# Hybrid decoder layer on one core: a set's own block in four tiles of its own, the second chain's first blocks unit by unit, and turns in two steps

## The chip, the cores and the metric

The kernel runs on one core of a Trainium2 chip. The metric is device time in microseconds (us), the time from the start to the end of one execution on the chip; lower is better. The engines are named as in the profile: PE multiplies matrices (PEld is its weight load), DVE and ACT work on tiles, POOL and SP mainly issue DMAs here, and POOL also does a few tiny powers.

## What is computed

One decoder layer on a sequence of 256 tokens with 2048 channels, all float32. Cut to what matters:

```python
h = rmsnorm(x, pre_norm_g)
proj = h @ w_in                       # one wide projection, split into the parts below
o_a = gla_chunked(a_q, a_k, a_v, gk)  # gated linear attention, 4 heads
y_a = (rmsnorm(o_a, gla_norm_g) * silu(a_g)) @ w_branch_a
o_b = diff_attention(b_q, b_k, b_v, lam)   # 16 heads, two softmaxes each
y_b = (rmsnorm(o_b, diff_norm_g) * silu(b_g)) @ w_branch_b
merged = sigmoid(m_a) * y_a + sigmoid(m_b) * y_b
out = x + rmsnorm(merged @ w_out, post_norm_g)
```

Nearly all of the work is the weight matrices: every weight is read once from HBM, split into a rounded part `hi` and a rest `lo`, and multiplied with the activations, which are split in the same way: hi by hi, hi by rest, rest by hi.

## The kernel before

**Units.** The weights go through the kernel in units of half a load. `schedule()` lists 452 units in the order in which PE takes them. `take()` hands PE one unit and prepares (`emit_half`) those up to four further on: `AHEAD = 4`. A regular unit is half of a 1 MB tile `raw` (three buffers), loaded by SP (L277). ACT makes `hi` of it (L298), DVE makes `lo` (L299), each in one of three buffers; PE then multiplies (L463, or L484 and L486 for channel-major parts).

**Sets.** Ten 512-column parts of the projection are computed in five pairs, "sets" 0 to 4, by seven products of half size in place of eight (a Strassen scheme). Each product has four units, and a set's 28 units are mixed in between the regular ones (the tuples in `steps`). ACT and DVE split a set unit in lines L259 and L260, PE multiplies it in L657. The blocks of weights that the products need are sums and differences of blocks. They are kept in two chains of four tiles of 512 KB: POOL loads a block into a chain tile (L213) or adds one to what is there (L211, an accumulating DMA), and DVE adds one chain tile to the other (L224). `refill()` is called when a unit is prepared; it puts the next load of the same tile on the list `refills`, from which it is issued two set units later.

The products of a set are p1, q3, p5, q6, q7, p2, p4 in sets 0, 3 and 4 and p1, q3, p5, p2, q6, q7, p4 in sets 1 and 2 (`MOVED`). One of them, p2, uses a block as it is, its "own block". In the kernel before, p2's block is loaded by SP in two halves of 1 MB into the same three `raw` buffers that the regular units use (L253, tile `raw_s`), and it is asked for when unit p2.0 or p2.2 is prepared. In sets 0, 3 and 4 DVE then adds it to a chain tile (L229), which p4 reads.

**Where these units stand.** In the list of units: v2 is units 16 to 23, v3 24 to 31, v4 32 to 44. `start_sets()` runs when unit 26 is prepared (while PE takes unit 22) and asks for the first blocks of set 0, p1 and q3, eight loads in a row; it does the same for set 1 at unit 173. Set 0's p1 units are 33, 35, 38 and 40, its q3 units 43, 45, 47 and 50, its p2 units 81 to 89. Set 3's q6 units are 312 to 318, its p2 units 328 to 334, in turn with units of y00 and y01. Set 4's q6 units are 368 to 374, in turn with units of y03; then come its four q7 units in a row (376 to 379), and p2 from 381 on.

**Buffers.** `u()` takes one of the 34 buffers of 4 KB per partition in the pool `big`; chain tiles, the split activations `xs`, the split sums `square`, the values `vh` and `vl`, the branch inputs `oah`, `oal`, `obh`, `obl` and the merged result `mh`, `ml` all live there. A buffer comes free when its tile's last reader is done. PSUM has eight banks, shared by everything.

**Order.** Each engine works through its own queue in order. The order in each queue is not written by hand: when the program is built, the framework takes for each engine the first instruction of the program that it works out to be ready, so an instruction can stand ahead of others that come earlier in the program. A wrong guess about when a load lands or a matmul ends is then fixed in the queue. `tc.keep_in_program_order` and `tc.issue_after` pin single instructions; the loads and refills of the chains are not pinned.

**v2 to v4.** After each of these parts `evacuate()` copies two PSUM banks, scaled, to `vh` (ACT, L556) and `vl` (DVE, L557). v2 holds columns 816 to 1231, so 208 of its columns end a tile `vh` and 208 begin the next one; only v2 has pieces of 208 columns. The forget gate's four PSUM banks are copied to `gp` by ACT (L532).

**The end.** `y1` is computed in four parts, y10 to y13, of eight units each. After y11 four small tasks run between the units (`pump`, after every second unit): `joined(0)` and `joined(1)` merge the first two parts, and `turn(g)` turns part g by eight transposes on PE (L1157) into two PSUM banks, from which ACT (L496) and DVE (L497) make `mh` and `ml`. Part 2 is turned by the task `turned(2)` in y13, part 3 by `turned(3)` in o0. Then the output projection o0 to o3 reads `mh` and `ml`.

Of the kernel before, what the change touches and what calls it, by code (L numbers as in the profile page):

```python
# [14 lines left out]
P = 128  # L15
# [125 lines left out]
def order_of(n):  # L141
    return ORDERS[n not in MOVED]
# [3 lines left out]
def hybrid_kernel(ctx: ExitStack, tc, xt, xn, preg, postg, w, w2, gkb, glag, lamv, diffg, ident_d, causal_d, lmask_d, out):  # L146
# [12 lines left out]
    def u(shape, name, dtype=F32):  # L159
        count[0] += 1  # L160
        return big.tile(shape, dtype, tag="u", name=f"{name}_{count[0]}")
# [9 lines left out]
    def ps(tag):  # L171
        count[0] += 1
        return psum.tile([P, 512], F32, tag="bank", name=f"{tag}_{count[0]}")
# [5 lines left out]
    def f32(ap):  # L179
        return ap.bitcast(F32)  # L180
# [13 lines left out]
    chains = [[], []]  # L194
# [3 lines left out]
    def piece(key, q):  # L198
        size = sizes[key]
        at = begins[key] + q * size * P  # L200
        return w[at : at + P * size].rearrange("(p n) -> p n", p=P)

    refills = []

    def block(n, name, unit, add=True):

        _, chain, (kh, g) = PRODUCTS[name]
        src = piece(SETS[n][g], 2 * kh + unit // 2)[:, 1024 * (unit % 2) : 1024 * (unit % 2) + 1024]
        dst = chains[(chain + n) % 2][unit]
        if add:  # L210
            pool.dma_start(dst, src, accum_op=ALU.add)  # L211
        else:
            pool.dma_start(dst, src)  # L213

    def refill(i, n, name, unit, raw):

        late = lambda *args, **kw: refills.append((i + 2, args, kw))
        x, y = chains[n % 2][unit], chains[(n + 1) % 2][unit]
        if name == "p1":
            late(n, "p5", unit)  # L220
        elif name == "p5" and n in MOVED:
            late(n, "q6", unit)
        elif name == "p5":
            dve.tensor_tensor(out=x, in0=x, in1=y, op=ALU.add)  # L224
            late(n, "q7", unit)
        elif name == "p2" and n in MOVED:
            late(n, "q7", unit)
        elif name == "p2":
            dve.tensor_tensor(out=x, in0=x, in1=raw, op=ALU.add)  # L229
        elif name == "q6" and n in MOVED:  # L230
            late(n, "p4", unit)
        elif name == "q7" and 0 < n < len(SETS) - 1:
            late(n + 1, "p1", unit, add=False)
        elif name == "p4" and 0 < n < len(SETS) - 1:
            late(n + 1, "q3", unit, add=False)
        while refills and refills[0][0] <= i:
            _, args, kw = refills.pop(0)
            block(*args, **kw)

    def emit_half():  # L240
        j = emitted[0]
        emitted[0] += 1
        key, unit = steps[j]
        if j in begin:
            start_sets()
        if isinstance(key, int):
            i = set_steps.index((key, unit))
            name, part = order_of(key)[unit // 4], unit % 4
            _, chain, (kh, g) = PRODUCTS[name]
            if chain is None:  # L250
                if part % 2 == 0:
                    raws[key] = wpool.tile([P, 2048], F32, tag="raw", name=f"raw_s{key}_{unit}")
                    sp.dma_start(raws[key], piece(SETS[key][g], 2 * kh + part // 2))  # L253
                raw = raws[key][:, 1024 * (part % 2) : 1024 * (part % 2) + 1024]
            else:
                raw = chains[(chain + key) % 2][part]
            hi_t = wpool.tile([P, 1024], F32R, tag="hi", name=f"hi_{j}")
            lo_t = wpool.tile([P, 1024], F32R, tag="lo", name=f"lo_{j}")
            act.activation(hi_t, raw, AF.Copy)  # L259
            dve.tensor_tensor(out=lo_t, in0=raw, in1=f32(hi_t), op=ALU.subtract)  # L260
            refill(i, key, name, part, raw)
            ready[j] = ((key, unit), hi_t, lo_t)
            return
        size = sizes[key]
        h = unit % 2
        src = piece(key, unit // 2)
        if h == 0:
            raws[key] = wpool.tile([P, 2048], F32, tag="raw", name=f"raw_{key}_{unit}")
        raw = raws[key]
        n = size // 2  # L270
        early = key == "v0"
        if h == 0:
            if j == 0:
                load_x(0, 1)
            cuts = (0, n, size) if j == 0 else (0, size)
            for a, b in zip(cuts, cuts[1:]):
                i = sp.dma_start(raw[:, a:b], src[:, a:b])  # L277
                if early:
                    tc.keep_in_program_order(i)
                if j == 0 and a == 0:  # L280
                    load_x(1, 3)
            if early:
                for kt in X_LOADS[j // 2]:
                    load_x(kt, 4)
        if early:
            prep_x(j)
            if 6 <= j < 14:
                square_x(j - 6)
        if key == "o3" and j + 1 < len(steps):
            hi_t, lo_t = u([P, 1024], "keep", F32R), u([P, 1024], "keep", F32R)  # L290
        else:
            hi_t = wpool.tile([P, 1024], F32R, tag="hi", name=f"hi_{j}")
            lo_t = wpool.tile([P, 1024], F32R, tag="lo", name=f"lo_{j}")
        fine = 2 if j == 0 else 1
        for i in range(fine):
            a, b = n * i // fine, n * (i + 1) // fine
            r = raw[:, n * h + a : n * h + b]
            act.activation(hi_t[:, a:b], r, AF.Copy)  # L298
            dve.tensor_tensor(out=lo_t[:, a:b], in0=r, in1=f32(hi_t[:, a:b]), op=ALU.subtract)  # L299
        ready[j] = (key, hi_t, lo_t)  # L300
# [23 lines left out]
    def load_x(kt, n):  # L324
        tc.keep_in_program_order(sp.dma_start(xraw[kt // 4][:, kt % 4 : kt % 4 + n, :], xt[:, kt : kt + n, :]))
# [4 lines left out]
    def prep_x(kt):  # L330
        i, j = kt // 4, kt % 4
        src = xraw[i][:, j, :]
        g = preg_s[:, kt : kt + 1]
        hi, lo = x_ops(kt)
        act.activation(hi, src, AF.Copy, scale=g)
        dve.scalar_tensor_tensor(out=lo, in0=src, scalar=g, in1=f32(hi), op0=ALU.mult, op1=ALU.subtract)
# [3 lines left out]
    def square_x(i):  # L340
        src = xraw[i // 2][:, 2 * (i % 2) : 2 * (i % 2) + 2, :].rearrange("p a t -> p (a t)")
        t = t2([P, 512], "xsq") if i else ssum
        tc.keep_in_program_order(act.activation(t, src, AF.Square))
        if i:
            dve.tensor_tensor(out=ssum, in0=ssum, in1=t, op=ALU.add)
# [149 lines left out]
    def split_out(bank, hi, lo, gain):  # L495
        act.activation(hi, bank, AF.Copy, scale=gain)  # L496
        dve.scalar_tensor_tensor(out=lo, in0=bank, scalar=gain, in1=f32(hi), op0=ALU.mult, op1=ALU.subtract)  # L497
# [125 lines left out]
    def start_sets():  # L623
        n = started[0]
        started[0] += 1
        while "squares" not in done:
            with tc.issue_after(latest[0]):
                next(operands, None)
        if n:
            for name, far in parts_far.items():  # L630
                parts[name] = tuple(u([P, 8, P], "square", F32R) for _ in far)
                for t, src in zip(parts[name], far):
                    pool.dma_start(f32(t), src)
        for c in range(2):
            chains[c][:] = [u([P, 1024], f"chain{c}") for _ in range(4)]
        for name in ("p1", "q3"):
            for unit in range(4):
                block(n, name, unit, add=False)

    def block_set(n, use):  # L640

# [87 lines left out]
    def late():  # L729
        norm_row()  # L730
        yield
        lam()
        yield
# [401 lines left out]
    first, both, raw = {}, {}, {}  # L1135
# [15 lines left out]
    def turn(g):  # L1151
        for i in range(2):
            bank = ps("bg")
            for j in range(2):
                for b in range(2):
                    c = P * (2 * i + j)
                    pe.transpose(bank[:, P * (2 * j + b) : P * (2 * j + b) + P], both[g][:, b, c : c + P], ident)  # L1157
            hi = mh[g][:, 2 * i : 2 * i + 2, :].rearrange("p a t -> p (a t)")
            lo = ml[g][:, 2 * i : 2 * i + 2, :].rearrange("p a t -> p (a t)")
            split_out(bank, hi, lo, 0.5)  # L1160

    def joined(g):
        yield from first_part(g)
        t = both[g]
        dve.scalar_tensor_tensor(out=t, in0=t, scalar=1.0, in1=raw[g], op0=ALU.add, op1=ALU.mult)
        dve.tensor_tensor(out=t, in0=t, in1=first[g], op=ALU.add)
        yield
        turn(g)

    def turned(g):  # L1170
        yield
        turn(g)

    for g in range(4):
        banks = token_major(f"y1{g}", 512, b_ops, 4)
# [145 lines left out]
```

## Time and profile before

| | us |
|---|---|
| median of 3 runs | 1120.77 |
| lowest and highest | 1120.32, 1121.54 |
| the profiled execution | 1120.19 |
| its span in the trace | 1118.4 |
| DVE, ACT, POOL busy | 817.2, 677.4, 136.2 |
| mean granted PE clock | 0.998 |

The span runs from the first to the last instruction in the trace; the profiled execution's time is 1.8 us longer than its span. Times in the timeline are in us from the start of the span; the second column is the duration of the row, which may hold several instructions (the xN at its end); in brackets stands how long the engine sat idle before it and what ended that. A row of DMA issues tells when the DMA was asked for, not when it landed.

### The profile page before, as it was taken

To read this page: it belongs to the slowest core of one execution; us is meant where nothing else is said; L and a number is where in the kernel's file an instruction comes from. 1 tells how busy PE (TensorE), PEld (TensorE's weight loads), DVE (VectorE), ACT (ScalarE), POOL (GpSimd) and SP (SyncE) were. 2 spreads that over 40 slices of the span, in tenths; PEclk is the share of its full clock that TensorE was granted. 3 is DMA by queue.
4 is the path that set the end of the run, shared out by engine and by line. 5 is a ranking of instruction groups with operands and counts; after the bars stand their busy time and mean duration, and the time that the engine had idled before them with its cause. 6 is when DMAs were issued, how large, how long until landed. Compare 5 with 4: busy or idle time off the path is not lost.

```text
span 1118.4 us, 15160 instructions
## 1 busy us (share of the span) xinstructions
PE 1103.1 (99%) x5578; PEld 947.6 (85%) x5578; DVE 817.2 (73%) x1151; ACT 677.4 (61%) x1003; POOL 136.2 (12%) x209
## 2 busy tenths in 40 slices
PE   9999999999999999999999999999999999999997
PEld 8999888888888888888888888888888878888886
DVE  7787769976776576568788878878676766585554
ACT  7868455554555566566778777776555555534451
POOL 0121000010001030022212302112112100000000
PEclk9999999999999999999999999999999999999999
DMA  8889754677566499489788978798788776588552
GB/s 324 256 334 298 224 177 131 237 279 297 210 237 214 144 358 366 162 206 246 224 283 221 243 235 256 263 313 235 258 301 253 199 286 234 193 336 314 186 208 76
DMA packets 55371, 274.56 MB, mean 245 GB/s; under 512 B 6848, under 2 KB 7488, under 8 KB 36608
## 3 DMA queue, kind: packets, MB, share of 16 engines
q1 hardware_dynamic: 33392, 195.97, 48.5%
q0 software_dynamic: 21184, 76.56, 25.7%
q10 hardware_dynamic: 720, 1.06, 0.3%
q8 instruction: 44, 0.72, 0.2%
q14 instruction: 31, 0.25, 0.1%
HBM read 249.44 MB, written 24.12 MB: 245 GB/s over the span
## 4 chain that ended last, share of the span: by engine, by line
PE 93%; issue 2%; DVE 2%; DMA 1%; ACT 1%; POOL 0%; SPq 0%; DVEq 0%; POOLq 0%; ACTq 0%
PE mm L463 47%; PE set L657 16%; PE mm L484 15%; PE mm L486 8%; PE bg L463 2%; PE mm L445 1%; PE bg L811 1%; DMA raw_s<-in_w_dram 1%; PE bg L445 1%; PE bg L939 1%; PE bg L940 1%; DMA raw_v<-in_w_dram 0%; DVE lo L260 0%; PE bg L965 0%; ACT hi L298 0%
## 5 line engine op out<-in xcount | busy, mean ns | idle before, releaser
L463 PE MATMUL mm<-hi,xs 128*128 128x512 f32 (+2 forms) x896 | 215.3, 380 | 2.8 <-DVE vl L557 1.7
L484 PE MATMUL mm<-xs,hi 128*128 128x512 f32 x768 | 198.1, 391 | 0.0
L260 DVE TENSOR_TENSOR lo<-chain,hi 128x1024 fp32r<-128x1024 f32 x120 | 146.4, 1223 | 63.7 <-ACT hi L259 62.4
L463 PEld LDWEIGHTS mm<-hi,xs 128*128 128x128 f32 x896 | 166.2, 188 | 28.7 <-DVE vl L557 2.1
L259 ACT ACTIVATE hi<-chain 128x1024 fp32r<-128x1024 f32 x120 | 127.0, 1061 | 95.9 <-PE mm L463 41.9
L484 PEld LDWEIGHTS mm<-xs,hi 128*128 128x128 f32 x768 | 142.0, 188 | 27.1 <-ACT hi L298 0.3
L463 PE MATMUL mm<-lo,xs 128*128 128x512 f32 (+2 forms) x448 | 116.1, 378 | 0.0
L486 PEld LDWEIGHTS mm<-xs,lo 128*128 128x128 f32 x768 | 104.7, 190 | 7.6
L486 PE MATMUL mm<-xs,lo 128*128 128x256 f32 x768 | 107.0, 282 | 0.0
L299 DVE TENSOR_TENSOR lo<-raw_y,hi 128x1024 fp32r<-128x1024 f32 x64 | 78.1, 1223 | 37.5 <-ACT hi L298 37.5
L298 ACT ACTIVATE hi<-raw_y 128x1024 fp32r<-128x1024 f32 x64 | 67.7, 1061 | 55.8 <-PE mm L463 30.1
L463 PEld LDWEIGHTS mm<-lo,xs 128*128 128x128 f32 x448 | 83.7, 188 | 13.0 <-DVE lo L299 0.3
L657 PE MATMUL set<-hi,square 128*128 128x512 f32 x320 | 86.9, 393 | 0.0
L211 POOL DMA_DIRECT2D chain<-in_w_dram x56 | 49.2, 879 | 211.6 <-DVE lo L260 108.4
L657 PEld LDWEIGHTS set<-hi,square 128*128 128x128 f32 x320 | 58.2, 189 | 10.3 <-ACT hi L259 0.4
L657 PE MATMUL set<-hi,xs 128*128 128x512 f32 x240 | 65.3, 393 | 0.0
L298 ACT ACTIVATE hi<-raw_ag 128x1024 fp32r<-128x1024 f32 x32 | 33.9, 1061 | 39.9 <-PE mm L463 35.8
L299 DVE TENSOR_TENSOR lo<-raw_ag,hi 128x1024 fp32r<-128x1024 f32 x32 | 39.1, 1223 | 21.4 <-ACT hi L298 21.2
L657 PE MATMUL set<-lo,square 128*128 128x512 f32 x160 | 49.8, 392 | 2.0 <-DVE lo L260 1.9
L463 PE MATMUL mm<-hi,obh 128*128 128x512 f32 x128 | 50.0, 391 | 0.8 <-ACT hi L298 0.8
L657 PEld LDWEIGHTS set<-hi,xs 128*128 128x128 f32 x240 | 43.8, 188 | 7.6
L299 DVE TENSOR_TENSOR lo<-raw_o,hi 128x1024 fp32r<-128x1024 f32 x25 | 30.6, 1225 | 26.7 <-ACT hi L298 26.6
(272 smaller groups left out, 2064.8 us busy)
## 6 DMA issues: line engine op xcount, KB each, us to landing
chain<-in_w_dram POOLq DMA_DIRECT2D x96, 512.0 KB, 8.8
raw_y<-in_w_dram SPq DMA_DIRECT2D x32, 1024.0 KB, 6.4
raw_ag<-in_w_dram SPq DMA_DIRECT2D x16, 1024.0 KB, 5.0
raw_dq<-in_w_dram SPq DMA_DIRECT2D x16, 1024.0 KB, 5.3
raw_dk<-in_w_dram SPq DMA_DIRECT2D x16, 1024.0 KB, 7.4
raw_o<-in_w_dram SPq DMA_DIRECT2D x16, 1024.0 KB, 4.9
raw_v<-in_w_dram SPq DMA_DIRECT2D x15, 832.0 KB, 5.8
raw_s<-in_w_dram SPq DMA_DIRECT2D x10, 1024.0 KB, 6.6
```

The lines of the kernel that those rows point to most:

```text
L211: pool.dma_start(dst, src, accum_op=ALU.add)
L259: act.activation(hi_t, raw, AF.Copy)
L260: dve.tensor_tensor(out=lo_t, in0=raw, in1=f32(hi_t), op=ALU.subtract)
L298: act.activation(hi_t[:, a:b], r, AF.Copy)
L299: dve.tensor_tensor(out=lo_t[:, a:b], in0=r, in1=f32(hi_t[:, a:b]), op=ALU.subtract)
L445: i = pe.matmul(out, lhs, rhs, start=first and n == 0, stop=last and n == len(pairs) - 1)
L463: i = pe.matmul(banks[g][b][:, :n], a[part][:, P * b : P * b + P], w[:, c : c + n], start=first, stop=last)
L484: i = pe.matmul(o, hi[:, c], x_pair(kt), start=kt == 0, stop=kt == KT - 1)
L486: i = pe.matmul(o[:, :S], lo[:, c], x_ops(kt)[0], start=False, stop=False)
L657: i = pe.matmul(bank, a[part], wt[:, 512 * j : 512 * j + 512], start=go, stop=end, skip_group_check=not first)
L811: pe.matmul(o, xk[:, P * c : P * c + P], xq.rearrange("p (b c t) -> p b c t", b=2, c=4)[:, :, c, :], start=i == 0, stop=i == 1)
L939: pe.matmul(banks[m][:, lo:up], q2[:, m, i2, t], kh[:, m, i2, :n], start=True, stop=False)
```

## The change

It has three parts.

1. **The own block of sets 0, 3 and 4.** When a unit of q6 is prepared, a tile `plain` is taken from the 34 buffers, and a POOL load of 512 KB into it is put on the list of refills, to be issued two set units later. p2 then reads this tile (and DVE adds it to the chain tile) in place of the half of a 1 MB `raw_s`. Sets 1 and 2 keep `raw_s`.
2. **q3's first blocks of sets 0 and 1.** `start_sets()` asks for p1's four blocks alone. q3's block is asked for when the p1 unit of the same number is prepared.
3. **Turns in two steps.** `turn(g)` becomes a generator that yields after each of its two banks for g below 3, so that a pump does four transposes of a part, and the next pump the other four. Part 3 is turned in one step as before.

```diff
     refills = []
+    plain = {}
 
     def block(n, name, unit, add=True):
         _, chain, (kh, g) = PRODUCTS[name]
         src = piece(SETS[n][g], 2 * kh + unit // 2)[:, 1024 * (unit % 2) : 1024 * (unit % 2) + 1024]
-        dst = chains[(chain + n) % 2][unit]
+        dst = chains[(chain + n) % 2][unit] if chain is not None else plain[n, unit]
...
         if name == "p1":
+            if n < 2:
+                block(n, "q3", unit, add=False)
             late(n, "p5", unit)
...
         elif name == "q6" and n in MOVED:
             late(n, "p4", unit)
+        elif name == "q6":
+            plain[n, unit] = u([P, 1024], "plain")
+            late(n, "p2", unit, add=False)
...
-            if chain is None:
+            if (key, part) in plain and name == "p2":
+                raw = plain.pop((key, part))
+            elif chain is None:
                 if part % 2 == 0:
                     raws[key] = wpool.tile([P, 2048], F32, tag="raw", name=f"raw_s{key}_{unit}")
...
-        for name in ("p1", "q3"):
-            for unit in range(4):
-                block(n, name, unit, add=False)
+        for unit in range(4):
+            block(n, "p1", unit, add=False)
...
             split_out(bank, hi, lo, 0.5)
+            if g < 3:
+                yield
...
-        turn(g)
+        yield from turn(g)
 
     def turned(g):
         yield
-        turn(g)
+        yield from turn(g)
```

## Prediction

> **What bounds the kernel now.** I read the page first, for the busy shares.
>
> ```profile
> span 1118.4 us, 15160 instructions
> ...
> PE 1103.1 (99%) x5578; PEld 947.6 (85%) x5578; DVE 817.2 (73%) x1151; ACT 677.4 (61%) x1003; POOL 136.2 (12%) x209
> ```
>
> PE is busy for 1103.1 of 1118.4 us and the change takes no matmul away. Start and tail stay as they are, so all that can be won is PE's waiting in between. The view of waits, for PE alone, names nearly all of it (engine, line, what it waited for, us in total, times, longest):
>
> ```profile
> PE mm L463 <- ACT hi L298: 1.9, 3, 0.8
> PE set L657 <- DVE lo L260: 1.9, 1, 1.9
> PE mm L463 <- DVE vl L557: 1.7, 1, 1.7
> ```
>
> Three waits of 1.9, 1.7 and 0.8 us are worth following. Their true price is a little higher: a 512-column matmul counts as busy for 0.39 us, but in a row of four (1.07 us) the next starts (1.07 - 0.39) / 3 = 0.227 us later, so each wait costs about 0.16 us more than the view says: 2.05, 1.87 and 0.97 us, 4.9 in sum. That is the ceiling, 0.4% of the time.
>
> *The wait of 1.9 us* is in set 4. The timeline there:
>
> ```profile
> 898.87 0.33 SPq L253 DMA_DIRECT2D raw_s<-in_w_dram  x1
> ...
> 902.87 1.06 ACT L259 ACTIVATE hi<-chain 128x1024 fp32r<-128x1024 f32 x1 [1.21 <-PE mm L463]
> ...
> 907.66 1.07 PE L657 MATMUL set<-hi,square 128*128 128x512 f32 x4
> 908.20 1.23 DVE L229 TENSOR_TENSOR chain<-chain,raw_s 128x1024 f32<-128x1024 f32 x1 [5.28 <-DMA raw_s<-in_w_dram]
> 909.34 1.22 DVE L260 TENSOR_TENSOR lo<-chain,hi 128x1024 fp32r<-128x1024 f32 x1
> ...
> 910.62 0.74 PE L657 MATMUL set<-lo,square 128*128 128x512 f32 x2 [1.89 <-DVE lo L260]
> ```
>
> The reader is to see a queue order that was guessed wrong. DVE's L229 needs the own block asked for at 898.87, and sits 5.28 us for it. Behind it stands the `lo` of q6.3, whose `hi` was done at 902.87 + 1.06 = 903.93: it starts 5.4 us late, and PE, which has begun q6.3 with its `hi`, loses 2.05. So some 5.4 - 2.05 = 3.4 us of lateness are covered by the units prepared ahead.
>
> *The wait of 1.7 us* is at the start of v4:
>
> ```profile
> 63.26 0.73 ACT L556 ACTIVATE vh<-mm,rstd 128x208 fp32r<-128x208 f32 x2
> ...
> 64.86 4.27 POOL L213 DMA_DIRECT2D chain<-in_w_dram  x8
> ...
> 81.94 1.17 ACT L556 ACTIVATE vh<-mm,rstd 128x208 fp32r<-128x208 f32 x3
> ...
> 82.98 1.21 ACT L532 ACTIVATE gp<-bg,gkb_s 128x256 f32<-128x256 f32 x3
> ...
> 83.46 0.88 PE L463 MATMUL mm<-hi,xs 128*128 128x400 f32 x3 [1.71 <-DVE vl L557]
> ```
>
> Only v2 has pieces of 208 columns. Its first half was copied at 63.26, the second, from the same two banks, at 81.94, and the gate's `gp` after that. v2's two banks, v3's two and the gate's four are all eight, so v4 gets none until DVE has read v2's second half. What did that half lack? Its source was ready at 63.26, so I take it to be the new buffer for the next `vh`. In the program the eight loads of set 0's chains come ahead of it (`start_sets` runs while PE takes unit 22, the copy after unit 23), and `gp` too comes after them. My reading: buffers are given out in program order, and eight chain tiles had to get theirs first, at the rate at which POOL's queue was reckoned to issue the loads.
>
> *The wait of 0.8 us* is at the first turns. ACT's timeline, then PE's (its last row is the turn of part 2):
>
> ```profile
> 996.90 1.09 ACT L496 ACTIVATE mh<-bg 128x512 fp32r<-128x512 f32 x2 [8.44 <-PE bg L1157]
> 997.87 2.01 ACT L298 ACTIVATE hi<-raw_y 128x1024 fp32r<-128x1024 f32 x2
> ```
>
> ```profile
> 996.26 1.91 PE L1157 MATMUL bg<-ident,mgate 128*128 128x128 f32 x16
> 998.98 0.50 PE L463 MATMUL mm<-hi,obh 128*128 128x512 f32 x1 [0.81 <-ACT hi L298]
> ...
> 1010.01 1.04 PE L1157 MATMUL bg<-ident,mgate 128*128 128x128 f32 x8
> ```
>
> Again an order: ACT sits 8.44 us in front of two `mh` that need transposes, with the `hi` of y13's first unit behind them. PE has used up its prepared units when the transposes come.
>
> **The change part by part.** *The own blocks.* Six of SP's ten L253 loads go, 1 MB each; twelve POOL loads of 512 KB come. The work of ACT, DVE and PE is the same, and so are the bytes. What a load costs:
>
> ```profile
> chain<-in_w_dram POOLq DMA_DIRECT2D x96, 512.0 KB, 8.8
> ...
> raw_s<-in_w_dram SPq DMA_DIRECT2D x10, 1024.0 KB, 6.6
> ```
>
> ```profile
> L213 POOL DMA_DIRECT2D chain<-in_w_dram x8: 540/551/551, 795.3 to 840.2; - x8
> ...
> DMA to landing us min/median/max: 3.9/5.1/8.1
> ```
>
> ```profile
> DMA to landing us min/median/max: 3.8/8.8/18.7
> ```
>
> First come the page's medians from issue to landing; then the view of the chain tiles between 790 and 846 us, the stretch of set 3's p2; then the same view over the whole run. Twelve issues of 0.55 us add 6.6 us to POOL's 136, hidden in a queue that is 12% busy (6.6 us is what they could cost at most if it were not). Behind them in it stand other chain loads, and in set 0 stores of `vh`; the attention's small powers run in sets 1 and 2, where no own block moves. SP loses six issues, and the regular units get back a `raw` buffer for as long as each `raw_s` held one. The Trainium skill speaks against this move: "DMA: Bandwidth & Descriptors", section "SWDGE vs HWDGE vs iDMA", sends plain transfers to SP or ACT, and its "Rules for kernel authors" want 1 MiB or more in a DMA. The medians agree in direction, though most of POOL's 96 loads accumulate; by that rule the sum would get nothing here.
>
> Set 4: eight buffers are free when its blocks are asked for: two that nothing holds, four `xs` last read by p1, and two `square` last read by q3. Four blocks and the first four `obh`/`obl` take them. The blocks then wait neither for a `raw` buffer nor for p2's preparation: they are asked for from unit 372 on, or earlier where POOL is free, against 381. I take the wait as gone: **-2.05 us** (bounds 0 and -2.05). What is late next is nothing: the four q7 units take 1.36 us each on PE (six matmuls of 0.227), and DVE's `lo` takes 1.22.
>
> Set 3: `xs`, `square`, the chains and `oah`/`oal` hold eight each, 32 of 34, so blocks 0 and 1 get buffers at once, and blocks 2 and 3 only when 0 and 1 have been split:
>
> ```profile
> 810.09 1.23 DVE L260 TENSOR_TENSOR lo<-raw_s,hi 128x1024 fp32r<-128x1024 f32 x1 [1.04 <-ACT hi L259]
> ```
>
> ```profile
> 817.21 1.06 ACT L259 ACTIVATE hi<-raw_s 128x1024 fp32r<-128x1024 f32 x1 [0.54 <-PE mm L463]
> ```
>
> p2.0's `lo` ends at 811.32, p2.2's `hi` starts at 817.21. With this stretch's 3.9 to 8.1 us the block lands at 815.2 to 819.4, at worst 2.2 us late, under the cover of 3.4: **0** (bounds 0 and the rival below). Block 3 follows in the same rhythm. POOL, which waits in order for the buffer, has set 4's chain loads behind it; p1's first is due with unit 344, sixteen units after p2.0. Set 0: 28 of 34 buffers are held (`xs`, `square` and chains 24, `gp` 2, `k`, `q`), so four fit: 0.
>
> *q3 unit by unit.* Eight issues (sets 0 and 1) move behind p1's units, POOL's stores of `vh` and the copies of v2. In set 0 only four chain tiles now stand ahead of v2's second half and `gp`. If these come four issues earlier, ACT has room for them (it idles before each `hi`), the banks are free at 81.6, and the wait goes: **-1.87 us** (bounds 0, if the buffers are not the reason, and -1.87). I take the lower end, since nothing else ties the second half to 81.94. The cover for the later loads: q3's first unit is prepared ten units after p1's (43 against 33).
>
> *Turns.* The 32 transposes stay. At 996 PE would do eight of the first sixteen, and the other eight after y13's second unit. If ACT's order stays (two `mh`, then `hi`), y13 still starts at 998.98, because ACT's chain sets that start; the eight that ran in the shadow of the wait now run outside it, 1.91 - 1.04 = 0.87 us. If `hi` comes first, the wait of 0.97 goes. The bounds are +0.87 and -0.97. I take **+0.87**, since two `mh` are ready after eight transposes as they were before. `mh` of part 2 is complete one pump later, six units ahead of its use in o0: 0.
>
> Sum: -2.05 - 1.87 + 0.87 = -3.05 us. The profiled execution (1120.19: span 1118.4 and 1.8 around it) would become 1117.14. The median of the runs is 0.58 above it, so 1120.77 - 3.05 = **1117.7 us**.
>
> **The rivals.**
> - *A better order at the turns*, both waits gone: -2.05 - 1.87 - 0.97 = -4.9, 1115.9 us. For it: one load decides which comes first. Against: the row of 8.44 us.
> - *The copies of v2 do not wait for buffers of the chains*, or the moved loads are drawn forward again, being pinned to nothing: 1120.77 - 2.05 + 0.87 = 1119.6. For it: the queue orders are only inferred.
> - *Set 4's own blocks are as late as before* (POOL still has q7's loads to issue): 1120.77 - 1.87 + 0.87 = 1119.8. This is also where the rule of the Trainium skill on plain transfers ("DMA: Bandwidth & Descriptors") leads.
> - *The change does not do what it says*: both waits stay, 1120.8 to 1121.6.
> - *Slower: set 3's missing buffers.* Blocks 2 and 3 start only at 811.32. With a landing of L us, p2.2 is L - 5.9 late and PE loses L - 5.9 - 3.4 = L - 9.3. At the run's longest, 18.7, that is 9.4 us: 1117.7 + 9.4 = 1127.1. It makes the kernel slower than before by 2.24 us from L = 9.3 + 3.05 + 2.24 = 14.6 on. Against it: the 8.1 of that stretch.
>
> **How the numbers follow.** A difference of 0.2% (2.24 us) is about what a measurement of this kernel can tell from none. The forecast has 0.36, the better order 0.15, the buffers not the reason 0.23, set 4 late 0.09, nothing done 0.07, set 3 slower 0.10. Faster: 0.36 + 0.15 = 0.51; same: 0.23 + 0.09 + 0.07 = 0.39; slower: 0.10. The range 1115.4 to 1121.8 reaches from the better order to "nothing done"; it leaves out the slower case and the scatter beyond the ends.
>
> **What would show it.** In the waits of PE, "set L657 <- DVE lo L260" and "mm L463 <- DVE vl L557" are gone. The 128x208 rows of L556 lie before 80 us, four chain loads stand in a row at 65. L229 no longer waits for a DMA in set 4. At the turns, PE waits about 1.7 us before y13 and the x16 row has become two of x8. I am wrong if L229 or L259 waits for `plain` in set 3 and PE behind it, if the copies still stand near 82, or if another wait of a microsecond has appeared.

## The result, and the profile after

| | before | after |
|---|---|---|
| median, in the same session (6 runs each) | 1121.41 us | 1125.12 us |
| lowest and highest | 1120.32, 1123.04 | 1124.72, 1126.81 |
| span of the profiled execution | 1118.4 us | 1125.0 us |

The ratio is 1.0039 (95% interval 1.0029 to 1.005; it is worked out over all the runs, while the two medians alone give 1.0033). By the medians the change makes the kernel 3.7 us slower, where 3 us less was forecast. The profiled execution is the slowest of the six, and that of before lies at its fast end, so what is read from the two is an upper size; the span is 6.6 us longer than that of before.

The page of the changed kernel, its busy shares:

```profile
span 1125.0 us, 15162 instructions
...
PE 1106.0 (98%) x5578; PEld 952.6 (85%) x5578; DVE 818.4 (73%) x1151; ACT 679.1 (60%) x1003; POOL 142.6 (13%) x221
```

POOL has its twelve issues and 6.4 us more, as counted. The other engines do the same work. PE's busy time is 2.9 us longer for the same 5578 matmuls, which its clock will explain below; the other 3.7 of the 6.6 us are waiting. The view of waits, PE alone:

```profile
PE mm L471 <- DVE lo L307: 6.6, 1, 6.6
PE mm L471 <- ACT hi L306: 2.4, 2, 1.7
```

The line numbers have moved by 1 to 8: L471 is what was L463, L307 the `lo` of a regular unit (L299), L267 and L268 `hi` and `lo` of a set unit (L259, L260), L232 DVE's addition of the own block (L229), L212 and L214 POOL's loads (L211, L213). L1035 is POOL's store of a finished `obh` or `obl`. Two of the three waits that the prediction named are gone: that of set 4 (`set <- lo`) and that at v4 (`mm <- vl`). The one at the turns has grown from 0.8 to 1.7 us. And there is one of 6.6 us that was not there. The chain of work that ended last, in the stretch from 760 to 800 us (start, duration, what), says where it comes from:

```profile
768.83 10.12 DMA obh_far<-obh
...
779.54 7.91 DMA plain<-in_w_dram
...
787.54 0.09 DVE chain L232
...
788.68 1.23 DVE lo L307
...
789.96 2.08 PE mm L471 x4
```

For 18 us the path that sets the end does not run over PE but over two DMAs in a row: the store of a finished tile `obh` to HBM, then the load of set 3's first own block. The timeline of the same place has the engines' side:

```profile
768.83 0.57 POOL L1035 DMA_DIRECT2D obh_far<-obh  x1 [1.65 <-ACT obh L504]
770.18 0.55 POOL L1035 DMA_DIRECT2D obl_far<-obl  x1 [0.78 <-DVE obl L505]
...
777.01 1.06 ACT L306 ACTIVATE hi<-raw_y 128x1024 fp32r<-128x1024 f32 x1 [0.75 <-PE set L664]
...
779.54 0.56 POOL L214 DMA_DIRECT2D plain<-in_w_dram  x1 [7.33 <-PE mm L471]
...
781.65 0.55 POOL L214 DMA_DIRECT2D plain<-in_w_dram  x1 [0.50 <-issue]
...
787.54 1.22 DVE L232 TENSOR_TENSOR chain<-chain,plain 128x1024 f32<-128x1024 f32 x1 [10.03 <-DMA plain<-in_w_dram]
788.68 1.22 DVE L307 TENSOR_TENSOR lo<-raw_y,hi 128x1024 fp32r<-128x1024 f32 x1
...
789.96 2.08 PE L471 MATMUL mm<-lo,oah 128*128 128x512 f32 x4 [6.64 <-DVE lo L307]
```

Read from the bottom. PE needs the `lo` of y00's first unit. That `lo` had its `hi` at 777.01 + 1.06 = 778.07, and stands on DVE behind L232, which adds set 3's first own block to a chain tile although p2 and p4 are still tens of microseconds away. L232 sits 10.03 us for the load. The load is issued only at 779.54, half a microsecond after the store of `obh` has landed (768.83 + 10.12 = 778.95). The wait of 7.33 us is put down to an instruction of PE there; three runs below name the store.

This is the same fault as the one that was removed from set 4 (an addition too early in DVE's queue, a `lo` behind it), moved to set 3 and made more than three times as long. Around it the clock falls. PE's row of the view by stretches (stretch, length, busy us and instructions of PE, PEld, DVE, ACT, POOL, granted PE clock, DMA share, GB/s), first after, then before:

```profile
780.00:790.00 10.00, 3.36 (x16) 2.47 (x14) 2.46 (x3) 2.44 (x5) 2.62 (x5) 0.92 1.00 308
790.00:794.60 4.60, 4.60 (x11) 3.65 (x12) 4.33 (x4) 1.88 (x2) 0.00 (x0) 0.50 0.07 27
```

```profile
770.00:780.00 10.00, 10.00 (x45) 8.26 (x44) 8.84 (x9) 5.80 (x6) 2.89 (x4) 1.00 1.01 316
780.00:790.00 10.00, 10.00 (x46) 8.27 (x45) 5.71 (x6) 6.35 (x7) 1.13 (x2) 1.00 1.04 332
790.00:794.60 4.60, 4.60 (x22) 3.82 (x21) 2.97 (x3) 2.23 (x3) 0.00 (x0) 1.00 0.31 77
```

For 4.6 us after the wait PE runs at a granted clock of 0.50 and does 11 matmuls where it did 22. If each of the 11 takes twice its 0.227 us, that is 11 x 0.227 = 2.5 us more, an estimate that fits the 2.9 us of busy time. Besides, the DMA engines were fully taken from 770 to 790 us before the change already (share 1.01 and 1.04), which a look at PE alone does not show.

The other places that the prediction named, in the timeline after:

```profile
66.26 2.14 POOL L214 DMA_DIRECT2D chain<-in_w_dram  x4
...
76.66 0.76 ACT L564 ACTIVATE vh<-mm,rstd 128x208 fp32r<-128x208 f32 x2
...
77.30 3.03 ACT L540 ACTIVATE gp<-bg,gkb_s 128x256 f32<-128x256 f32 x8
```

Four chain loads stand in a row in place of eight, and v2's second half is copied at 76.66 in place of 81.94.

### The profile page after: what moved, and what is told of

It reads as the page before. It is cut to its first block, busy times and chain, and to the rows that moved or that the text cites. A ratio compares the mean times of both kernels' runs of the same rounds, so it can differ in the third digit from the quotient of the medians.

```text
span 1125.0 us, 15162 instructions
## 1 busy us (share of the span) xinstructions
PE 1106.0 (98%) x5578; PEld 952.6 (85%) x5578; DVE 818.4 (73%) x1151; ACT 679.1 (60%) x1003; POOL 142.6 (13%) x221
## 3 DMA queue, kind: packets, MB, share of 16 engines
q10 hardware_dynamic: 720, 1.06, 0.3%
## 4 chain that ended last, share of the span: by engine, by line
PE 92%; issue 2%; DMA 2%; DVE 1%; ACT 1%; POOL 0%; POOLq 0%; DVEq 0%; SPq 0%; ACTq 0%
PE mm L471 46%; PE set L664 16%; PE mm L492 15%; PE mm L494 7%; PE bg L471 2%; PE mm L453 1%; PE bg L818 1%; DMA obh_far<-obh 1%; PE bg L453 1%; DMA plain<-in_w_dram 1%; PE bg L946 1%; PE bg L947 1%; PE bg L972 0%; DMA raw_v<-in_w_dram 0%; PE bg L890 0%
## 5 line engine op out<-in xcount | busy, mean ns | idle before, releaser
L471 PE MATMUL mm<-hi,xs 128*128 128x512 f32 (+2 forms) x896 | 215.8, 381 | 0.7 <-ACT hi L306 0.7
L268 DVE TENSOR_TENSOR lo<-chain,hi 128x1024 fp32r<-128x1024 f32 x120 | 146.4, 1223 | 59.8 <-ACT hi L267 59.5
L267 ACT ACTIVATE hi<-chain 128x1024 fp32r<-128x1024 f32 x120 | 126.8, 1059 | 103.3 <-PE mm L471 42.0
L471 PEld LDWEIGHTS mm<-hi,xs 128*128 128x128 f32 x896 | 167.3, 189 | 25.7 <-ACT hi L306 1.0
L471 PE MATMUL mm<-lo,xs 128*128 128x512 f32 (+2 forms) x448 | 116.5, 379 | 0.0
L307 DVE TENSOR_TENSOR lo<-raw_y,hi 128x1024 fp32r<-128x1024 f32 x64 | 78.1, 1224 | 35.6 <-ACT hi L306 35.5
L471 PEld LDWEIGHTS mm<-lo,xs 128*128 128x128 f32 x448 | 84.0, 188 | 13.0 <-DVE lo L307 0.3
L212 POOL DMA_DIRECT2D chain<-in_w_dram x56 | 49.2, 878 | 205.2 <-DVE lo L268 117.4
L307 DVE TENSOR_TENSOR lo<-raw_ag,hi 128x1024 fp32r<-128x1024 f32 x32 | 39.2, 1224 | 24.1 <-ACT hi L306 23.9
L471 PE MATMUL mm<-hi,obh 128*128 128x512 f32 x128 | 50.2, 393 | 1.7 <-ACT hi L306 1.7
L307 DVE TENSOR_TENSOR lo<-raw_o,hi 128x1024 fp32r<-128x1024 f32 x25 | 30.6, 1226 | 26.8 <-ACT hi L306 26.7
L471 PE MATMUL mm<-hi,oah 128*128 128x512 f32 x128 | 50.1, 391 | 0.0
```

What stands on the lines that cost most here:

```text
L471: i = pe.matmul(banks[g][b][:, :n], a[part][:, P * b : P * b + P], w[:, c : c + n], start=first, stop=last)
```

## The experiments

**Theory A**: the loss is set 3's alone. Its plain tiles get buffers only when the stores of `obh` and `obl` have landed, and DVE's addition stands ahead of a `lo`. Against it stand **B**, that more loads through POOL's queue make its loads late in general; **C**, that the load is too late for its own unit, wherever the addition stands; and **D**, that it takes the other two parts of the change to make it late. All times below are medians; ratios are against the kernel before in the same session, with 95% intervals.

**Set 3 without plain tiles.**

```diff
-        elif name == "q6":
+        elif name == "q6" and n != 3:
             plain[n, unit] = u([P, 1024], "plain")
```

> Both other parts stay, and sets 0 and 4 keep their four plain tiles; only set 3 goes back to the raw_s tiles of before. Theory A (set 3's plain tiles get their buffers only when the stores of obh and obl have landed, and a DVE addition that waits for them stands ahead of a lo): the wait of 6.6 us behind L307 is gone, PE has no wait over 2.4 us, and the sum of the prediction is left, -2.05 - 1.87 + 0.87 = -3.05 us against before, ratio 0.997. Rival B (more loads through POOL's queue make its loads late in general): eight of the twelve loads are still there, a PE wait of several us behind a plain or chain load stays somewhere, ratio 1.000 or more.

1117.01 against 1121.4 us, 0.9966 (0.9953 to 0.9979). PE's waits:

```profile
PE mm L471 <- ACT hi L306: 2.1, 2, 1.7
PE bg L387 <- DVE ones L384: 1.0, 1, 1.0
```

Only the wait at the turns (1.7) and the start are left. Eight plain loads are still on POOL, so B falls for these loads; the forecast's sum holds once set 3 is left out. POOL's timeline has more to say:

```profile
777.07 0.56 POOL L214 DMA_DIRECT2D plain<-in_w_dram  x1 [6.12 <-DMA obh_far<-obh]
```

This load is one of set 4's: its place is not pinned, and now it stands where set 3's first block stood, waiting for the same store. DVE first reads a plain tile of set 4 near 890 us, so here the late load costs nothing.

**The addition in program order.**

```diff
-            dve.tensor_tensor(out=x, in0=x, in1=raw, op=ALU.add)
+            tc.keep_in_program_order(dve.tensor_tensor(out=x, in0=x, in1=raw, op=ALU.add))
```

> All of the change, but the addition of the own block to the chain (L232) keeps its place in program order on DVE, behind the lo of the same unit. The loads are as in the changed kernel. Theory A: plain 3.0 is still issued only when the stores have landed and lands about 19 us after them (near 787 us), but p2.0 is due near 810, so no lo stands behind the wait and PE does not wait: -3.05 us, ratio 0.997. Rival C (the load is late enough to be missed by its own unit, whatever DVE's order): the wait moves to p2's hi in set 3 and PE loses 2 us or more there, ratio 0.999 to 1.003. Rival B (POOL's queue): a wait of several us stays, ratio over 1.000.

1117.69 us, 0.9966 (0.9954 to 0.9978). The timeline:

```profile
779.52 0.56 POOL L214 DMA_DIRECT2D plain<-in_w_dram  x1 [6.95 <-DMA obh_far<-obh]
...
809.27 1.23 DVE L268 TENSOR_TENSOR lo<-plain,hi 128x1024 fp32r<-128x1024 f32 x1 [1.04 <-ACT hi L267]
810.41 1.22 DVE L232 TENSOR_TENSOR chain<-chain,plain 128x1024 f32<-128x1024 f32 x1
```

The load is issued as late as in the changed kernel (779.52), and the profile now names the store as what held it for 6.95 us. But it is first read near 808 us, so its lateness costs nothing: C falls. The addition runs at 810.41 without waiting. With the addition out of the way the late load does no harm; what costs is the addition's place in DVE's queue.

**The own blocks alone** (q3's loads and the turns as before).

> The kernel before with only the own blocks on plain tiles; q3's loads and the turns as before. Theory A: the loss in set 3 belongs to this part by itself. Set 4's wait of 1.9 us is gone (-2.05), set 3's of 6 to 7 us and the slow clock behind it come; with the medians the part is the changed kernel's +3.7 less the other two parts (-1.87 + 0.87), so +4.7 us, ratio 1.004. Rival D (it takes q3's moved loads or the later turns to make the loads of set 3 late): -2.05 us, ratio 0.998.

1124.96 us, 1.0042 (1.0026 to 1.0058), +4.7 us by the ratio: this part alone makes the loss, and D falls. The waits, and POOL's row:

```profile
PE mm L469 <- DVE lo L305: 5.0, 1, 5.0
```

```profile
779.99 0.56 POOL L214 DMA_DIRECT2D plain<-in_w_dram  x1 [6.87 <-DMA obh_far<-obh]
```

The wait is 5.0 us here and 6.6 in the profile of the whole change: it is as long as two DMAs happen to take, and differs between the two profiles.

**The turns alone** (two steps in `turn`, all else as before).

> The kernel before with only the turns in two steps. By the prediction's step: ACT still does two mh ahead of the hi of y13, eight transposes leave the shadow of the wait, +0.87 us, ratio 1.0008, PE's wait at y13 about 1.7 us. Rival: the hi comes first and the wait goes, -0.97 us, ratio 0.9991.

1122.37 us, 1.0009 (1.0 to 1.0017). The waits:

```profile
PE mm L463 <- ACT hi L298: 2.6, 3, 1.7
```

The longest of them is the 1.7 us at y13, as worked out: 0.81 before, and 1.91 - 1.04 = 0.87 more. The median's +1.0 us agrees, though its interval touches no change.

**q3's loads alone** (the two edits in `refill` and `start_sets`).

> The kernel before with only the loads of q3 moved behind p1's units. By the prediction's step (buffers are given out in program order, and eight chain tiles stand ahead of v2's second half): the wait of 1.7 us at v4 is gone, -1.87 us, ratio 0.9983; the other waits stay. Rival (the copies of v2 hang on something else): the wait stays, 1.000.

1118.77 against 1121.52 us, 0.9977 (0.9968 to 0.9986). PE's waits are those of before without the one at v4 (`mm <- vl`):

```profile
PE set L658 <- DVE lo L262: 2.1, 2, 1.9
PE mm L465 <- ACT hi L300: 1.7, 3, 0.8
```

**Eight loads in a row, but later.** This asks whether it was the number of loads or their place in the program.

```diff
-    begin = {steps.index((n, 0)) - 7 for n in (0, 1)}
+    begin = {steps.index((n, 0)) - (5, 7)[n] for n in (0, 1)}
```

> The kernel before, with set 0's eight chain loads still in one row but asked for two units later, behind the copies of v2. By the prediction's reading (buffers are handed out in program order, the chain tiles stand ahead of vh and gp): the wait of 1.7 us at v4 is gone, -1.87 us, ratio 0.9983, the copies of 208 columns lie before 80 us. Rival (eight loads in one row hold up something by their number): the wait stays, 1.000.

1122.51 against 1121.26 us, 1.0007 (0.9998 to 1.0016): a miss in the time. In the trace the mechanism shows. The timeline, then PE's waits:

```profile
65.75 0.76 ACT L556 ACTIVATE vh<-mm,rstd 128x208 fp32r<-128x208 f32 x2
...
66.02 3.73 POOL L213 DMA_DIRECT2D chain<-in_w_dram  x7
```

```profile
PE mm L463 <- ACT hi L298: 1.9, 5, 0.8
PE set L657 <- DVE lo L260: 1.8, 1, 1.8
PE set L657 <- ACT hi L259: 1.1, 1, 1.1
```

The copies stand ahead of the eight loads, at 65.75 (the eighth load is issued at 70.88), and the wait at v4 is gone. So the copies were held by what comes ahead of them in the program. In its place come a wait of 1.05 us in set 0's first product and two of 0.23 us shortly before it (86.58 and 89.25 in PE's timeline; the first row counts five waits where there were three). With 0.16 us each for PE's pitch they make 2.0 us, about the whole gain of 1.87.

**The addition in program order, in the kernel before** (the same edit on L229, with `raw_s` as it was).

> The kernel before, with raw_s and all loads as they were; only the addition L229 keeps its place in program order on DVE. If the place of the addition in DVE's queue is what costs, and not the late load, set 4's wait of 1.9 us goes without any earlier load: -2.05 us, ratio 0.9982. Rival (the load as such is late): the wait moves from the lo of q6.3 to a hi or lo of p2 and 1 us or more stays, ratio 0.999 to 1.000.

1118.36 against 1121.52 us, 0.9974 (0.9964 to 0.9985). PE's waits:

```profile
PE mm L463 <- ACT hi L298: 2.2, 3, 1.0
PE mm L463 <- DVE vl L557: 1.7, 1, 1.7
```

Set 4's wait is gone, without any load asked for earlier: the own block is asked for at 899.54, in the kernel before at 898.87.

**The whole change with the addition in program order and the turns as before.**

> The changed kernel with L232 in program order and with the turns in one step again. If the terms add up: -2.05 - 1.87 = -3.92 us, ratio 0.9965, PE's longest wait behind the start of 0.8 to 1.0 us, at y13.

1117.06 us, 0.9961 (0.9949 to 0.9974). Of the three waits the one at y13 is left, 0.81 us in PE's timeline and 0.97 by its pitch.

**The same with ACT's `mh` in program order.**

```diff
-            split_out(bank, hi, lo, 0.5)
+            tc.keep_in_program_order(act.activation(hi, bank, AF.Copy, scale=0.5))
+            dve.scalar_tensor_tensor(out=lo, in0=bank, scalar=0.5, in1=f32(hi), op0=ALU.mult, op1=ALU.subtract)
```

> As the run with the turns as before, but ACT's mh of the turns keep their place in program order too, behind the hi of y13's first units. By the prediction's second-best case the wait of 0.97 goes as well: -4.9 us, ratio 0.9956. Rival (the mh come so late that something behind them, the o products or the lo of y13 behind ml on DVE, waits): a new wait of about 1 us, ratio 0.9965 or more.

1115.61 us, 0.9948 (0.9936 to 0.9961). ACT's timeline:

```profile
990.53 2.01 ACT L306 ACTIVATE hi<-raw_y 128x1024 fp32r<-128x1024 f32 x2 [5.64 <-DMA raw_y<-in_w_dram]
992.95 1.07 ACT L306 ACTIVATE hi<-raw_y 128x1024 fp32r<-128x1024 f32 x1 [0.42 <-PE mm L471]
996.49 1.06 ACT L306 ACTIVATE hi<-raw_y 128x1024 fp32r<-128x1024 f32 x1 [2.47 <-PE mm L471]
997.46 1.06 ACT L1167 ACTIVATE mh<-bg 128x512 fp32r<-128x512 f32 x2
```

The `hi` of y13 start at 990.53 and no longer stand behind the `mh`. Behind the start the view of waits has none of PE's over 0.2 us.

**One more buffer.** The pool u gets 35 buffers (the small t2 tiles 6 for 8).

> The changed kernel with 35 in place of 34 buffers in the pool u (the small t2 tiles get 6 instead of 8 to make room). Theory A (set 3's plain tiles wait for buffers that obh and obl hold until their stores land): plain 3.0 now finds a buffer at once and is issued near 773 us, not 779.5; only plain 3.1 and 3.2 still wait for the stores. The order on DVE stays, so a shorter wait is left, of the second addition: its load is issued near 779.5, lands near 787, and is wanted one pair of units (4.1 us) after the first, near 782, 5 us late with 3.4 covered: PE waits 1 to 4 us instead of 6.6, ratio 0.998 to 1.002. Rival B (POOL loads are late in themselves, whatever buffer): PE waits 6 us or more as before, ratio 1.003 or more.

1120.03 against 1121.26 us, 0.9989 (0.9979 to 0.9998). POOL's and DVE's rows:

```profile
767.75 0.85 POOL L214 DMA_DIRECT2D plain<-in_w_dram  x1
...
778.40 1.22 DVE L232 TENSOR_TENSOR chain<-chain,plain 128x1024 f32<-128x1024 f32 x1
...
780.61 0.56 POOL L214 DMA_DIRECT2D plain<-in_w_dram  x1 [7.53 <-PE mm L471]
...
787.27 1.23 DVE L232 TENSOR_TENSOR chain<-chain,plain 128x1024 f32<-128x1024 f32 x1 [4.83 <-DMA plain<-in_w_dram]
```

With a buffer in hand the first block is asked for at 767.75, and the first addition does not wait. The second block is now the one that goes out at 780.61, just after the store of `obh` has landed (issued at 769.68, 10.1 us to the landing), and PE waits 1.4 us:

```profile
PE mm L471 <- DVE lo L307: 1.4, 1, 1.4
```

With 0.16 for the pitch that is -3.05 + 1.6 = -1.45 us, and the ratio says -1.2 (interval -2.4 to -0.2): theory A's size. The buffers, not POOL, made the load late. PE also has two waits of 0.8 us in sum in the attention (L947) that no other run has; whether they come of the fewer t2 tiles was not tested.

**The orders only**: the kernel before with q3's loads behind p1's units, L229 and the `mh` in program order, no plain tile, turns in one step.

> The kernel before without any plain tile and with the turns in one step: only q3's loads behind p1's units, the addition L229 in program order on DVE, and the mh of the turns in program order on ACT. If the three waits were all matters of order, and the earlier loads of the own blocks buy nothing: -2.05 - 1.87 - 0.97 = -4.9 us, ratio 0.9956, like the version with twelve plain tiles (0.9948, interval 0.9936 to 0.9961). Rival (the earlier loads are worth something by themselves): a wait of 1 us or more in set 3 or 4, ratio 0.9965 or more.

1115.06 against 1121.26 us, 0.9947 (0.9933 to 0.996). The largest PE waits behind the start:

```profile
PE bg L812 <- DVE xk L795: 0.4, 1, 0.4
PE bg L940 <- ACT kh L921: 0.2, 1, 0.2
```

It is as fast as the version with plain tiles (0.9948, each against the kernel before in its own session): the twelve earlier loads are worth nothing that can be measured with intervals some 0.0026 wide. This is the version to keep, 0.5% below the kernel before.

## Why the prediction was wrong

**What bounds the kernel**: right. All gains and losses are PE's waits and, behind the longest of them, its clock, and the three waits named were all there was to win: with all three gone the two best versions take 5.8 and 5.9 us off by the ratio (the interval of 0.9933 to 0.996 holds the ceiling of 4.9). The seven runs whose gain had been forecast as a sum of stalls came out 0.4 to 1.1 us beyond that sum, by the ratio. Each interval holds its sum, but all lie on one side, and why stays open.

**Set 4's own blocks, -2.05**: the wait went as forecast. But the remedy was not the earlier load. The step had quoted the right row (DVE sits 5.28 us with a `lo` behind) and called it a queue order guessed wrong; the addition put in order removes the wait with the load as late as it was. One sign did not come as written: in set 4 L232 still waits once for a DMA, 1.65 us at 910.95 in the profile after, though PE does not wait for it.

**Set 3, "blocks 0 and 1 get buffers at once": this is the step that failed.** It counted 32 of 34 buffers by tiles that compute reads, and took the other two as free. They had last held `obh` and `obl`, whose last readers are the stores of 768.83 and 770.18, and these held them for 10 to 11 us more. So the first block went out at 779.54, and DVE's addition of it, drawn ahead of y00's `lo`, made PE wait 6.6 us: the term was not 0. For blocks 2 and 3, the ones that the step worried about, the landing of 3.9 to 8.1 us sufficed: ACT waited 1.0 and 1.3 us for them, PE not at all. Two further things are missing in that step. It has no landing for blocks 0 and 1. Its 3.9 to 8.1 us are from 790 to 846 us, while these two loads fall into the stretch before, where the DMA share was 1.01 and 1.04; there they took 7.9 and 9.6 us, and for the three accumulating loads of the kernel before, the view of the chain tiles from 765 to 790 us has

```profile
DMA to landing us min/median/max: 10.6/12.3/12.9
```

And it asked whether the load comes in time for p2, but not where DVE's addition of it would be put. That the framework puts such an addition early was known from set 4, from the row of 5.28 us. The cover of 3.4 us, on the other hand, held: the `lo` came 788.68 - 778.07 = 10.6 us late, and PE's pitch shows 6.8 us lost, so 3.8 were covered.

**q3 unit by unit, -1.87**: right in size (the run alone gives -2.6, interval -1.6 to -3.6 us), and right that the loads' place in the program decides. That it does so through the buffers is the prediction's reading; no run tests that by itself.

**Turns, +0.87**: right, order and size.

**The rivals**: the slower one had the place (set 3's missing buffers) and not the mechanism. It put the missing buffers at blocks 2 and 3 and the loss at p2's `hi`, and gave it 0.10 for the short landings. The sign that the prediction gave for it, L229 waiting for `plain` in set 3 and PE behind it, is the one that came. Its price of up to 9.4 us came near by chance: the profiled execution lost 6.8 in the wait and 2.5 by the clock. The sum with these is -2.05 - 1.87 + 0.87 + 6.8 + 2.5 = +6.25 us, against +6.6 between the two spans. For the medians (+3.7) set 3's term is 3.7 + 3.05 = 6.8 us.

The rule of the Trainium skill on plain transfers ("DMA: Bandwidth & Descriptors", section "SWDGE vs HWDGE vs iDMA") did not decide the case: set 4's wait went, and with the addition in order the plain loads through POOL cost nothing that could be measured (0.9948 with them, 0.9947 without).

## What to carry to other kernels

When a tile is to be loaded earlier, ask for the buffer first: who held it last, and if that was a store to HBM, when the store lands, at the DMA share of that very stretch. Then follow every instruction that reads the new tile to its place in its engine's queue, not only the one for which the tile was moved. Where the profile shows an engine sitting in front of work that isn't due, put that instruction in its place before moving loads about.

## What the hardware showed besides

PE's granted clock halves after a long pause. After the wait of 1.9 us in set 4 (before) it stays at 1.00; after that of 5.0 us (own blocks alone) and of 6.6 us (after) it is 0.50. In this order:

```profile
910.60:915.00 4.40, 4.38 (x19) 3.61 (x20) 4.40 (x5) 1.46 (x2) 0.00 (x0) 1.00 0.52 153
```

```profile
789.50:792.50 3.00, 3.00 (x8) 2.31 (x8) 2.81 (x3) 0.85 (x1) 0.00 (x0) 0.50 0.23 93
```

The row of after, from 790.00 to 794.60, stands above. So in this profile a wait of 6.6 us costs some 9 (6.8 by PE's pitch and 2.5 by the clock). The Trainium skill ("TensorE: Matmul & The Clock Gate", section "What's actually happening") says that the clock drops to half after an idle window of about 3.4 us and comes back after a busy one. The pauses on both sides of that figure agree; the 4.6 us at half clock are more than one such window.

A store holds its buffer far longer than its issue suggests: 0.57 us on POOL, 10.12 us to the landing, in a stretch with a DMA share near 1 (1.02 from 770 to 780 us after the change).
